# Handing out the attention's score steps in turn with the transposes and value products of other blocks

## The chip, the cores and the metric

The kernel runs on one core of one Trainium2 chip. A time is the device time of one execution in microseconds (us). The kernel before was timed three times: the median is 1233.09 us, the runs reach from 1231.47 to 1233.61. Engines are named as the profile names them: PE (matrix products), PEld (its weight loads), DVE (vector), ACT (scalar, activation functions), POOL (GpSimd) and SP (issues the DMAs).

## The reference

Two layers of a transformer trunk over a sequence of 512 tokens of width 1024, in float32. Each layer has two kinds of attention heads side by side, which share one input projection and one output projection, and then a dense MLP:

```python
proj = einsum('bsd,de->bse', rmsnorm(x, attn_norm[l]), w_in[l])
sb_q, sb_k, sb_v, df_q, df_k, df_v = split(proj, ...)      # 512 columns each
# stick-breaking: 8 heads of 64
z = q @ k.T * d**-0.5
log_keep = where(kpos < qpos, log_sigmoid(-z), 0.0)
between = cumsum(log_keep, reverse=True) - log_keep
w = where(kpos < qpos, exp(log_sigmoid(z) + between), 0.0)
sb_out = w @ v
# differential: 4 heads, two maps each of 64, values of 128, rotary positions on q and k
p = softmax(where(kpos // 64 <= qpos // 64, q @ k.T * d**-0.5, -inf))   # for both maps
df_out = rmsnorm((p[0] - lam * p[1]) @ v, subln_norm[l]) * (1 - lambda_init)
x = x + concat([sb_out, df_out]) @ w_o[l]
x = x + square(relu(rmsnorm(x, mlp_norm[l]) @ w_ff1[l])) @ w_ff2[l]
```

After both layers there is one final norm.

## The kernel before

Everything is held transposed, with features on the 128 partitions and the 512 tokens along the free axis. Each float32 operand of a product is split into a high part (rounded by ACT, `whi`, `h_hi`) and the remainder (by DVE, `wlo`, `h_lo`), and a product is three matmuls (function `three`, L255 to L260): high by high, and the two mixed ones. Weights come in units of 128 by 1024 numbers, loaded by SP (L106) and split one or two units ahead of use (L118 on ACT, L119 on DVE).

In each layer the attention is worked at the same time as the input projection. Two Python generators hand out work in steps. `dense()` (L693) goes through the projection's column blocks in the order d0, w0, d1, w1, ..., s0, u0, ...: d are queries and keys of a differential head, w its values, s and u the same of a pair of stick-breaking heads. One step of it is three matmuls of 512 columns (0.648 of the planner's units of cost). `attn()` (L652) yields attention steps with costs of 0.2 to 0.65. After each dense step the loop at L727 adds to a credit that is capped at 0.1, and while it is positive it takes the next attention step and subtracts its cost. A step that yields 0 is not ready: its queries and keys, or its values, are not due yet by the planner's clock, and the credit is dropped. Instructions recorded in this order are then ordered on each engine by the framework's scheduler, which follows this order by priority and its own notion of what is ready. On the chip each engine works through its own list in that order; waits are semaphores.

The attention of a layer is cut into 24 units: eight of the differential heads (4 heads times 2 halves of the queries) and sixteen of the stick-breaking heads (8 heads times 2 halves). A half has two query blocks of 128 tokens; block i sees 128(i + 1) keys. Work of a unit has three stages:

- `s1_df` or `s1_sb`, the scores: two matmuls into a PSUM bank of tag "s" (L487, L488), of which there are two. For a differential unit DVE then masks (L527, L531), takes the negated row maximum (L528, L532), ACT takes the exponential with its sum (L540), and DVE and POOL combine the two maps (L546 to L549). In the second half of a head (blocks 2 and 3) each map needs a bank of its own, so the unit has four score steps; in the first half two maps share one bank and there are two steps. For a stick-breaking unit ACT takes two sigmoids (L502, L503), DVE a product scan (L505) and POOL a product (L508); there are two steps.
- `s2`, the transposes of the weights: PE transposes (L568) into a bank of tag "t" (two banks, shared with the values' transposes vT, L393, and with the norm's rs and rb), then ACT and DVE split them (L205, L206: `zh`, `zl`, `fh`, `fl`). One step in the first half, two in the second.
- `s3`, the products with the values (L596 to L600) into the one bank of tag "o". One or two steps.

For unit i, `attn()` runs all score steps of unit i, then s2 of unit i - 2, then s3 of unit i - 3. When a differential head is complete its norm is put in between: `start_norm` (L639: transposes rs of L229, sums on DVE, a power on POOL at L236, a cast `chi` on DVE at L237, two diagonal products on POOL) and, one unit later, `finish` (L644: the broadcast matmuls rb of L251 and L252, then a split).

Projections are evicted by DVE; for queries and keys of a differential head POOL applies the rotation (L459, L460), ACT and DVE split the result (`h0d2k`, `l0d2k`), SP moves the pieces into stacked tiles (L425) and ACT copies others (L446, `copy_k`).

A tile's name has its layer and block: S0d230 is the score tile of layer 0, differential head 2, query block 3, map 0. The profile leaves out the number at the end.

Of the kernel before, what the change touches and what calls it, by code (L numbers as in the profile page):

```python
# [31 lines left out]
LAG2, LAG3, KSB = 2, 3, 7  # L32
# [54 lines left out]
class _Weights:  # L87
# [42 lines left out]
    def next(self, kind):  # L130
        i = self.used
        assert _UNITS[i][0] in kind
        self.used += 1
        if i > 0:
            self.do_split(i + 2)
        return self.tiles.pop(i)
# [3 lines left out]
def trunk(ctx, tc, xT, w, gains, lamv, cos, sin, out):  # L140
# [6 lines left out]
    def bank(tag, name, bufs=2):  # L147
        return ps.tile([P, 512], F32, tag=tag, name=name, bufs=bufs)
# [55 lines left out]
    def split(hi, lo, src):  # L204
        nc.scalar.activation(hi, src, AF.Copy)  # L205
        nc.vector.tensor_tensor(out=lo, in0=src, in1=hi.bitcast(F32), op=ALU.subtract)  # L206
# [41 lines left out]
    def rms_b(bc, name, dg):  # L248
        dg_hi, dg_lo = dg
        pb = bank("t", "rb_" + name)  # L250
        nc.tensor.matmul(pb, ones_r.to_broadcast([P, P]), dg_hi, start=True, stop=False)  # L251
        nc.tensor.matmul(pb, ones_r.to_broadcast([P, P]), dg_lo, start=False, stop=True)  # L252
        nc.scalar.copy(bc, pb)

    def three(pt, a, b, first, last):  # L255
        ah, al = a
        bh, bl = b
        nc.tensor.matmul(pt, ah, bh, start=first, stop=False)  # L258
        nc.tensor.matmul(pt, ah, bl, start=False, stop=False)  # L259
        nc.tensor.matmul(pt, al, bh, start=False, stop=last)  # L260
# [88 lines left out]
    for l in range(L):  # L349
        with ExitStack() as actx:  # L350
# [18 lines left out]
            def tt(name):  # L369
                return a2.tile([P, S], F32, tag="t", name=name, bufs=4)  # L370
# [184 lines left out]
            def s2(u):  # L555
                half = u["half"]
                nm = f"{l}{u['kind']}{u['b']}{u['m']}{half}"
                u["wT"] = {}
                for bk in range(half + 1):
                    zed = bk == half  # L560
                    pt = bank("t", f"T{nm}{bk}")
                    for kk in (1, 0):
                        kb = 2 * bk + kk
                        for qi in range(2):
                            if kb > 2 * half + qi:
                                continue
                            off = (1 - kk) * 256 + qi * P
                            nc.tensor.transpose(pt[:, off : off + P], u["w"][qi][:, kb * P : (kb + 1) * P], ident)  # L568
                    if zed:
                        zh, zl = zt[zn[0] % 2]  # L570
                        zn[0] += 1
                        a = 128
                    else:
                        zh = a2.tile([P, 512], F32R, tag="fh", name="fh" + nm, bufs=1)
                        zl = a2.tile([P, 512], F32R, tag="fl", name="fl" + nm, bufs=1)
                        a = 0
                    split(zh[:, a:512], zl[:, a:512], pt[:, a:512])
                    if not zed:
                        yield 0.44
                    for kk in range(2):  # L580
                        u["wT"][2 * bk + kk] = (
                            zh[:, (1 - kk) * 256 : (2 - kk) * 256], zl[:, (1 - kk) * 256 : (2 - kk) * 256])
                yield 0.33

            def s3(u):
                half, b, m, kind = u["half"], u["b"], u["m"], u["kind"]
                key = (kind, b, m)
                if half == 0:
                    heads[key] = bank("o", f"O{l}{kind}{b}{m}", 1)
                o = heads[key][:, half * 256 : half * 256 + 256]  # L590
                n = 2 * half + 2
                for kb in range(n):
                    wh, wl = u["wT"][kb]
                    if kind == "s":
                        v = vs[:, kb, 2 * b + m, :]
                        nc.tensor.matmul(o, v, wh, start=(kb == 0), stop=False)  # L596
                        nc.tensor.matmul(o, v, wl, start=False, stop=(kb == n - 1))  # L597
                    else:
                        three(o, (vd_hi[:, kb, b * P : (b + 1) * P], vd_lo[:, kb, b * P : (b + 1) * P]), (wh, wl),
                              kb == 0, kb == n - 1)  # L600
                    if kb % 2 and kb < n - 1:
                        yield 2 * 256 * (2 if kind == "s" else 3) * MMC
                if half == 1:
                    o = heads.pop(key)
                    if kind == "s":
                        if m == 0:
                            heads[("mt", b)] = a2.tile([P, S], F32, tag="mt", name=f"mt{l}{b}", bufs=MTB)
                        mt = heads[("mt", b)]
                        oc = tt(f"oc{l}{b}{m}")[0:64, :]
                        nc.scalar.copy(oc, o[64:128, :])  # L610
                        nc.vector.tensor_add(mt[64 * m : 64 * m + 64, :], o[0:64, :], oc)
                        if m == 1:
                            split(ms_hi[:, b, :], ms_lo[:, b, :], mt)
                    else:
                        os_ = a2.tile([P, S], F32, tag="mt", name=f"os{l}{b}", bufs=MTB)
                        sqo = tt(f"sqo{l}{b}")
                        nc.scalar.activation(sqo, o, AF.Square)
                        nc.scalar.activation(os_, o, AF.Copy, scale=gsub[:, l : l + 1])
                        rc = a3.tile([P, 4], F32, tag="rc", name=f"rc{l}{b}")
                        late.append((b, os_, sqo, rc))  # L620
                yield 2 * 256 * (2 if kind == "s" else 3) * MMC

            units = []
# [10 lines left out]
            def ok(key):  # L634
                return ready.get(key, 1e9) <= clock[0]
# [3 lines left out]
            def start_norm():  # L639
                b, os_, sqo, rc = late[0]  # L640
                dgs[b] = rms_a(sqo, 1.0 / P, rc, f"d{l}{b}", nc.gpsimd, tr)
                return 0.43

            def finish():  # L644
                b, os_, _, _ = late.pop(0)
                rb = tt(f"rb{l}{b}")
                rms_b(rb, f"d{l}{b}", dgs[b])
                nc.gpsimd.tensor_mul(os_, os_, rb)
                split(md_hi[:, b, :], md_lo[:, b, :], os_)
                return 0.43  # L650

            def attn():  # L652
                n = len(units)
                stage = 0
                for i in range(n + LAG3):
                    stage = stage + 1 if late else 0
                    if i < n:
                        u = units[i]
                        while not ok((u["kind"], u["b"])):
                            yield 0  # L660
                        yield from (s1_sb if u["kind"] == "s" else s1_df)(u)
                    if stage == 1:
                        yield start_norm()
                    if 0 <= i - LAG2 < n:
                        yield from s2(units[i - LAG2])
                    if stage == 2:
                        yield finish()
                        stage = 0
                    if 0 <= i - LAG3 < n:
                        while not ok(("v" + units[i - LAG3]["kind"], units[i - LAG3]["b"])):  # L670
                            yield 0
                        yield from s3(units[i - LAG3])

            def wo(half):
                for j in range(4):
# [17 lines left out]
            def dense():  # L693
# [28 lines left out]
                yield from wo(1)  # L722

            at = attn()
            done = spent = credit = 0.0
            live = True
# [23 lines left out]
        with ExitStack() as fctx:  # L750
# [25 lines left out]
            for half in range(2):  # L776
# [15 lines left out]
                n = HC - END if fin else HC  # L792
                for db in range(KC):
                    pt = bank("mm", f"f2_{l}{half}{db}", 3)
                    for s in range(2):
                        u = W.next("2")
# [72 lines left out]
```

## Time and profile before

| what | value |
|---|---|
| median of three runs | 1233.09 us |
| the profiled execution | 1232.63 us |
| its span, first to last instruction | 1230.8 us |
| PE busy in the span | 1196.4 us (97%) |
| DVE, ACT, POOL busy | 683.6, 550.6, 210.9 us |
| granted PE clock, mean | 0.993 |
| attention of layer 0 | about 55 to 210 us |
| attention of layer 1 | about 650 to 810 us |

A row of a timeline gives the start and the duration in us, the engine, the line of the kernel, the operation, the output and inputs by name, and in brackets how long the engine sat idle before it and what released it. A row of the waits gives who waited for whom, the total in us, the number of times and the longest. Ends of matmuls are modelled: consecutive rows of PE overlap, so their starts say more than their durations.

In the stretch from 55 to 105 us PE is busy for 43.65 of 50 us, from 160 to 200 us for 37.41 of 40. From 800 to 1200 us, in the MLP, it is busy throughout.

### The profile page before, as it was taken

The page shows a single profiled execution, that of the slowest core. Times are in us where ns is not written, and L with a number is a line of the kernel's source. Part 1 is how long each engine was busy: PE and PEld are TensorE (multiplying, and loading weights), DVE is VectorE, ACT ScalarE, POOL GpSimd, SP SyncE. Part 2 cuts the span into 40 slices and gives each one's busy share as a digit, 9 for nine tenths or more (in the row PEclk, how much of TensorE's full clock was granted, in tenths as well). Part 3 has the DMA queues.
Part 4 walks back from the last instruction along what each step waited for, and adds up shares of the span by engine and source line. Part 5 has one row for each costly group of instructions (what it writes and reads, how often), then busy time and mean ns, then how long its engine had stood idle before and what let it go on. Part 6 is the DMA issues. An engine that isn't in the chain of part 4 may idle for free.

```text
span 1230.8 us, 15320 instructions
## 1 busy us (share of the span) xinstructions
PE 1196.4 (97%) x5658; PEld 989.4 (80%) x5658; DVE 683.6 (56%) x1009; ACT 550.6 (45%) x932; POOL 210.9 (17%) x267
## 2 busy tenths in 40 slices
PE   8999999999999999999998999999999999999996
PEld 4777888888888888888887788788888888888886
DVE  6687878765442244443367787887644323444325
ACT  5666566544332134333246765665443221433214
POOL 4223453230000000001123244432200000000002
PEclk9999999999999999999999999999999999999998
DMA  6444444123322323323324343432232233233221
GB/s 198 114 142 121 115 134 122 59 86 103 103 88 101 103 88 101 103 87 102 103 84 141 105 134 107 129 92 84 86 103 99 90 103 95 93 103 91 90 94 69
DMA packets 46890, 128.16 MB, mean 104 GB/s; under 512 B 7264, under 2 KB 10336, under 8 KB 46816
## 3 DMA queue, kind: packets, MB, share of 16 engines
q1 hardware_dynamic: 46672, 127.17, 33.8%
q8 instruction: 45, 0.74, 0.2%
q14 instruction: 29, 0.24, 0.1%
q10 hardware_dynamic: 144, 0.02, 0.0%
HBM read 104.09 MB, written 2.10 MB: 86 GB/s over the span
## 4 chain that ended last, share of the span: by engine, by line
PE 87%; DVE 4%; ACT 3%; POOL 2%; issue 1%; DMA 1%; SPq 0%; DVEq 0%; POOLq 0%; ACTq 0%
PE f L258 19%; PE f L259 19%; PE f L260 19%; PE wo L259 2%; PE wo L258 2%; PE wo L260 2%; DVE wlo L119 1%; PE T1s L568 1%; PE T0s L568 1%; ACT p0d L540 1%; PE O1s L597 0%; PE O0s L597 0%; PE O0s L596 0%; PE O1s L596 0%; PE S1d L487 0%
## 5 line engine op out<-in xcount | busy, mean ns | idle before, releaser
L118 ACT ACTIVATE whi<-raw 128x1024 fp32r<-128x1024 f32 (+2 forms) x200 | 205.1, 1027 | 493.3 <-PE f L259 427.6
L119 DVE TENSOR_TENSOR wlo<-raw,whi 128x1024 fp32r<-128x1024 f32 (+2 forms) x200 | 247.7, 1239 | 151.6 <-ACT whi L118 150.5
L258 PE MATMUL f<-h_hi,whi 128*128 128x512 f32 x512 | 199.4, 389 | 0.0
L260 PE MATMUL f<-h_hi,wlo 128*128 128x512 f32 x512 | 199.2, 389 | 0.0
L259 PE MATMUL f<-h_lo,whi 128*128 128x512 f32 x512 | 199.2, 389 | 0.0
L258 PE MATMUL f<-uh,whi 128*128 128x512 f32 x496 | 192.9, 389 | 0.0
L259 PE MATMUL f<-ul,whi 128*128 128x512 f32 x496 | 192.9, 389 | 0.0
L260 PE MATMUL f<-uh,wlo 128*128 128x512 f32 x496 | 192.9, 389 | 0.0
L771 DVE SCALAR_TENSOR_TENSOR ft<-f,rbc 128x512 f32<-128x512 f32 x64 | 44.3, 692 | 163.9 <-PE f L260 163.0
L258 PEld LDWEIGHTS f<-h_hi,whi 128*128 128x128 f32 x512 | 96.1, 188 | 20.0
L260 PEld LDWEIGHTS f<-h_hi,wlo 128*128 128x128 f32 x512 | 96.1, 188 | 20.0
L259 PEld LDWEIGHTS f<-h_lo,whi 128*128 128x128 f32 x512 | 96.1, 188 | 19.8
L223 POOL TENSOR_TENSOR ssq<-ssq,sq 128x512 f32<-128x512 f32 x28 | 44.5, 1591 | 382.1 <-ACT sq L222 372.7
L260 PEld LDWEIGHTS f<-uh,wlo 128*128 128x128 f32 x496 | 93.1, 188 | 19.5
L258 PEld LDWEIGHTS f<-uh,whi 128*128 128x128 f32 x496 | 93.1, 188 | 19.3
L259 PEld LDWEIGHTS f<-ul,whi 128*128 128x128 f32 x496 | 93.1, 188 | 19.2
L800 DVE TENSOR_TENSOR x<-x,f 128x512 f32<-128x512 f32 x32 | 22.0, 688 | 103.0 <-PE f L260 103.0
L340 POOL TENSOR_TENSOR ssq<-ssq,sqf 128x256 f32<-128x256 f32 x6 | 4.4, 738 | 338.4 <-ACT sqf L338 335.0
L206 DVE TENSOR_TENSOR ul<-fu,uh 128x512 fp32r<-128x512 f32 x64 | 44.1, 692 | 0.4 <-ACT uh L205 0.4
L205 ACT ACTIVATE uh<-fu 128x512 fp32r<-128x512 f32 x64 | 40.6, 634 | 2.0
L772 ACT ACTIVATE fu<-ft 128x512 f32<-128x512 f32 x64 | 39.6, 618 | 1.6 <-DVE ft L771 1.6
L508 POOL TENSOR_TENSOR sig0s<-sig0s,C0s 128x128 f32<-128x128 f32 (+3 forms) x32 | 30.1, 939 | 55.0 <-DVE C0s L505 39.0
(722 smaller groups left out, 2164.9 us busy)
## 6 DMA issues: line engine op xcount, KB each, us to landing
raw<-in_w SPq DMA_DIRECT2D x176, 512.0 KB, 3.4
raw<-in_w SPq DMA_DIRECT2D x16, 448.0 KB, 3.2
x<-in_xT SPq DMA_DIRECT2D x8, 256.0 KB, 4.5
out_xT<-y SPq DMA_DIRECT2D x8, 256.0 KB, 2.4
raw<-in_w SPq DMA_DIRECT2D x8, 128.0 KB, 4.5
cos_t<-in_cos SPq DMA_DIRECT2D x2, 256.0 KB, 4.2
sin_t<-in_sin SPq DMA_DIRECT2D x2, 256.0 KB, 4.3
kl0d0k<-l0d0k SPq DMA_DIRECT2D x8, 64.0 KB, 2.2
```

Of the source, the lines that this page charges most:

```text
L118: nc.scalar.activation(hi[:, a:b], raw[:, a:b], AF.Copy)
L119: nc.vector.tensor_tensor(out=lo[:, a:b], in0=raw[:, a:b], in1=hi[:, a:b].bitcast(F32), op=ALU.subtract)
L205: nc.scalar.activation(hi, src, AF.Copy)
L206: nc.vector.tensor_tensor(out=lo, in0=src, in1=hi.bitcast(F32), op=ALU.subtract)
L223: eng.tensor_tensor(out=ssq, in0=ssq, in1=sq, op=ALU.add)
L258: nc.tensor.matmul(pt, ah, bh, start=first, stop=False)
L259: nc.tensor.matmul(pt, ah, bl, start=False, stop=False)
L260: nc.tensor.matmul(pt, al, bh, start=False, stop=last)
L508: nc.gpsimd.tensor_mul(sig[:, 0:wd], sig[:, 0:wd], C[:, 1 : wd + 1])
L568: nc.tensor.transpose(pt[:, off : off + P], u["w"][qi][:, kb * P : (kb + 1) * P], ident)
L771: nc.vector.scalar_tensor_tensor(out=t, in0=pt, scalar=0.0, in1=rbc, op0=ALU.max, op1=ALU.mult)
L772: nc.scalar.activation(uu, t, AF.Square)
```

## The change

The body of `attn()` is rearranged. What follows a unit's scores (the norm's start, s2 of unit i - 2, the norm's finish, s3 of unit i - 3) becomes a generator of its own, `behind_scores`. After each score step of unit i one step of that generator is handed out; what is left of it follows after the last score step. A step of it that is not ready yet (0) is asked again until it is. Which steps there are, their costs and what each computes stay as they are.

```diff
+            def behind_scores(i, stage):
+                n = len(units)
+                if stage == 1:
+                    yield start_norm()
+                if 0 <= i - LAG2 < n:
+                    yield from s2(units[i - LAG2])
+                if stage == 2:
+                    yield finish()
+                if 0 <= i - LAG3 < n:
+                    while not ok(("v" + units[i - LAG3]["kind"], units[i - LAG3]["b"])):
+                        yield 0
+                    yield from s3(units[i - LAG3])
+
             def attn():
...
                     stage = stage + 1 if late else 0
+                    rest = behind_scores(i, stage)
                     if i < n:
                         u = units[i]
                         while not ok((u["kind"], u["b"])):
                             yield 0
-                        yield from (s1_sb if u["kind"] == "s" else s1_df)(u)
-                    if stage == 1:
-                        yield start_norm()
-                    if 0 <= i - LAG2 < n:
-                        yield from s2(units[i - LAG2])
+                        front = (s1_sb if u["kind"] == "s" else s1_df)(u)
+                        for cost in front:
+                            yield cost
+                            nxt = 0
+                            while nxt == 0:
+                                nxt = next(rest, None)
+                                if nxt is not None:
+                                    yield nxt
+                    yield from rest
                     if stage == 2:
-                        yield finish()
                         stage = 0
-                    if 0 <= i - LAG3 < n:
-                        while not ok(("v" + units[i - LAG3]["kind"], units[i - LAG3]["b"])):
-                            yield 0
-                        yield from s3(units[i - LAG3])
```

A unit's steps are therefore handed out as score, transposes, score, transposes or values, ..., where they were score, score, transposes, ..., values.

## The prediction

> **What bounds the kernel now.** The page's busy shares come first: PE is busy 97% of 1230.8 us, so only PE's idle time can be won. I then asked for what PE waited for, over the span:
>
> ```profile
> PE S0d L487 <- ACT p0d L540: 6.7, 5, 2.2
> PE S1d L487 <- ACT p1d L540: 6.4, 4, 3.0
> ...
> PE rb_d L251 <- DVE zl L206: 2.0, 2, 1.0
> ...
> PE T0s L568 <- DVE vs L401: 1.6, 1, 1.6
> PE T1s L568 <- DVE vs L401: 1.6, 1, 1.6
> ...
> PE T0d L568 <- DVE p0d L549: 0.4, 1, 0.4
> ```
>
> Score matmuls of the differential blocks ("d") wait for a score bank that an exponential has not read out (13.1 us). A broadcast matmul rb and a transpose T of the stick-breaking blocks ("s") wait for a "t" bank (5.2 us). All are in the attention stretches. Third, the timelines around the largest waits say why:
>
> ```profile
> 99.38 0.48 PE L258 MATMUL p0w3v<-h_hi,whi 128*128 128x512 f32 x1
> 102.10 0.50 PE L487 MATMUL S0d<-st0d2k,st0d2q 128*128 128x512 f32 x1 [2.23 <-ACT p0d L540]
> 98.78 0.63 ACT L205 ACTIVATE h0d3k<-u0d3q 128x512 fp32r<-128x512 f32 x1 [2.67 <-POOL u0d3q L459]
> 99.45 1.90 ACT L446 ACTIVATE st0d3k<-h0d3k 32x512 fp32r<-32x512 f32 x3
> 101.38 0.58 ACT L540 ACTIVATE p0d<-S0d,sm0d 128x384 f32<-128x384 f32 x1
> 96.43 2.32 POOL L459 TENSOR_TENSOR u0d3q<-u0d3q,v0d3k 128x512 f32<-128x512 f32 x1
> ```
>
> The exponential itself takes 0.58, but ACT works in order: it sat 2.67 us for POOL's rotation, then made three copies, and PE waited.
>
> ```profile
> 186.66 0.48 PE L258 MATMUL p0s3q<-h_hi,whi 128*128 128x512 f32 x1
> 186.98 0.39 PE L259 MATMUL p0s3q<-h_lo,whi 128*128 128x512 f32 x1
> 189.69 0.55 PE L568 MATMUL T0s<-edge,sig0s 128*128 128x128 f32 x3 [1.62 <-DVE vs L401]
> 187.31 1.75 DVE L505 TENSOR_TENSOR_SCAN C0s<-keep0s,edge 128x512 f32<-128x512 f32 x1
> 188.97 0.66 DVE L401 TENSOR_TENSOR vs<-vT0u,vs 128x512 fp32r<-128x512 f32 x1
> 166.69 1.95 DVE L119 TENSOR_TENSOR wlo<-raw,whi 128x1024 fp32r<-128x1024 f32 x1
> 168.57 0.54 DVE L206 TENSOR_TENSOR zl<-T0s,zh 128x384 fp32r<-128x384 f32 x1
> ```
>
> In the s blocks it is DVE's order: the small splits that free a bank stand behind a scan (1.75) or a weight split (1.95).
>
> The idle column understates a wait, since the end of the matmul before it is modelled. I count start to start: 512-column matmuls follow each other every 0.23 us, so 99.38 to 102.10 loses 2.72 - 0.23 = 2.49.
>
> **What is lost now where the change reaches.** Layer 0, block d1 (68 to 81 us): 1.49 at 69.98, 0.23 at 72.08, 0.56 at 74.61, 0.26 at 80.97, sum 2.54. d2: 0.49 at 96.17 and 2.49, 2.98. d3: 1.09 at 125.68. Layer 1: d1 0.98 (676.49), d2 2.25 (702.06), d3 0.69 (723.60). s blocks: 1.15 at 169.26 and 1.79 at 189.69, and the same at 769.36 and 789.79, 5.88. Together **16.4 us**. The first pair of wide scores of block d0 (1.90 idle at 59.89, 3.00 at 656.14) is issued before any transposes are due; its surroundings keep their order, so both waits stay.
>
> **The change, part by part.** Nothing is added or removed: each engine has as many instructions (PE 5658 matmuls), and SP issues as many DMAs; only order moves. Direct costs are therefore zero, with the matmul stream itself as cover, and everything is in the waits. SP still issues the 16 stack moves of a block in one group (0.59 each), past at most one weight load more or less; no PE wait names these moves now, and scores follow them by several us: nothing. Walking the built program's new order with the durations above gives:
>
> *s blocks (16 units a layer).* The first transposes of a unit now come before its second score. At 169.26 the split zl now stands ahead of the eviction t0s2q (0.68) and the weight split (1.95) on DVE, and the norm's transposes are 1.8 us of PE work earlier, so POOL's power (1.0) no longer holds the cast behind it back: wait 0 instead of 1.15. At 189.69 T now takes a bank freed by a split that stands before the 1.75 scan: the copy, the weight split and a 384-wide scan still precede it, leaving 0.6 instead of 1.79. Two layers: 1.2 instead of 5.88. The closest new spacing of two score tiles on one bank is 4.5 us (4.9 before) against a sigmoid pair of 0.6 + 0.6, so these add nothing; if ACT were held up, the cover is 3 us.
>
> *d2.* Scores of a pair now stand 2.2 us apart on PE instead of 0.6 to 1.0, with transposes and the norm between. Layer 0: the second score's maximum now waits on DVE behind the cast chi, which waits for POOL's power (1.0) behind the rotation (2.32 beside DVE work); its exponential then ends 0.85 after PE arrives. Further on, weight split 13 falls behind that block's last combination (0.74) and PE's s0k projection waits 0.9. Sum 1.75, against 2.98. Layer 1's order has the maximum before chi and the weight split before the exponential: 0.3, against 2.25.
>
> *d3.* The second exponential goes behind a transposes' split zh on ACT, and rb behind the sigmoid table load (1.28): 0.3 + 0.35 in each layer, 1.3 against 1.78.
>
> *d1.* Here the change speaks against itself. Layer 0: the 1.49 goes, because the rotation's copies move behind the exponentials. But v0d2k is formed later, so POOL's rotation (1.3) runs ahead of the last map's scaling (1.04) and DVE's combination (0.74): the next transposes wait 1.55, where they waited 0.56. Then the block's third wide score comes only 1.6 us of PE work after the first (2.7 before), which is what memset, maximum and exponential take (0.11 + 0.55 + 0.58 + 0.19) without any queue. On ACT a weight split (1.09) and two 0.6 splits are ahead: 1.15. Its partner follows 4.1 us later and still finds 4 copies and a weight split ahead: 0.65. Small ones (whi 0.4, others 0.45) make 4.2 against 2.54. Layer 1: ACT waits for the rotation u1d2q (2.3 beside a weight split) ahead of the exponential: 1.35 + 0.4 = 1.75 against 0.98.
>
> Sum after: 1.2 + 1.75 + 0.3 + 1.3 + 4.2 + 1.75 = **10.5**. Gain 16.4 - 10.5 = **5.9 us**. The profiled execution took 1232.63 (span 1230.8 + 1.8 around it), the median shown is 1233.09, 0.46 above. So 1232.6 - 5.9 = 1226.7 by the profile and **1227 us** as median.
>
> Each remaining wait could be 0 (bank already free) or twice its size (two queues late together): after between 0 and 21, time between 1216.7 and 1237.7. I take the walked values, since their rows are neighbours of the ones moved.
>
> [...] The granted clock was 0.50 from 657.0 to 660.4, right after the 3.00 us idle; matmuls came every 0.43 there, which cost 1.5 us. No wait walked above reaches 3 us, so the sum has no such stretch besides this one. [...]
>
> POOL's L459 took 1.30 at 67.30, and DVE's combination that began 0.08 later took 1.63 (0.60 at 82.56, with POOL idle); at 96.43, begun 0.04 after a weight split on DVE, L459 took 2.32. I used 2.3 in layer 0's d2. [...]
>
> **Rivals.**
> - *The waits only change place* (1230.5 to 1235.5): the s gain of 4.7 holds, but d1 to d3 lose 4.7 more than their 10.5 of now. For: d1 already loses more by my walk. Against: d2's large waits have a named cause that moves away.
> - *Slower, about 1236.* ACT and DVE are in order, and transposes' splits and the norm's cast now stand between the two exponentials of a pair. If this holds PE at every d1 to d3 as long as the longest wait of this kind seen (3.00 idle, 3.16 start to start), the six lose 19.0, plus 1.2 in s: 20.2 - 16.4 = +3.8, hence 1236.9; with a single 3 us wait that halves the clock, +1.5 more. It decides from a mean of (16.4 - 1.2) / 6 = 2.5 us a block. For: d1 of layer 0 is above that by my walk. Against: elsewhere the pair's spacing doubles.
> - *Everything opens up*: no d wait is left, 1.2 in s: 1233.1 - 15.2 = 1218. Against it speaks the 1.6 us spacing in d1.
> - *The words do nothing*: the instruction scheduler reorders by its own readiness and PE's order stays. Excluded from d1 on: PE's order differs through both attention stretches.
>
> **How the numbers follow.** Under 0.2% (2.5 us) a measurement of this kernel hardly tells from no change; the three runs span 2.1. Forecast (2.5 to 10 us faster) 0.55, everything opens up 0.08, waits only change place 0.15, slower 0.22. Faster 0.63, same 0.15, slower 0.22. The forecast alone: 1223 to 1230.5. Range for 8 in 10: 1221 to 1235.5, leaving out half of the best case and the worst third of the slower one.
>
> **What would show it.** In the new profile: no PE wait of rb_d for zl in either layer; T0s for a split under 1 us; d2's wait under 1 us in layer 1; a transposes' wait T0d for p0d of about 1.5 and score waits at d1; the 1.9 and 3.0 of d0 as before. Wrong would be: a 2 us score wait left in d2 or d3, a second stretch at clock 0.5, or weight splits ("wlo") as new releasers of projections over 1 us.

## The result, and the profile after

The changed kernel takes 1230.83 us (median of ten executions, 1228.94 to 1233.19), the kernel before in the same sitting 1234.14. The ratio is 0.9974, with a 95% interval from 0.9965 to 0.9983: 3.2 us faster, between 2.1 and 4.3. The forecast was 5.9 us and a time of 1227.

The profiled execution of the changed kernel is its slowest, 1233.19 us with a span of 1231.4. The waits of PE in it, by the view that the prediction began with (who waited for whom: us, times, longest):

```profile
PE S1d L487 <- ACT p1d L540: 4.2, 2, 3.0
PE S0d L487 <- ACT p0d L540: 3.6, 3, 2.0
...
PE rb_d L251 <- DVE vs L401: 1.6, 2, 0.8
...
PE T0d L568 <- DVE p0d L549: 1.3, 2, 1.1
...
PE rb_d L251 <- DVE vdl L401: 1.0, 1, 1.0
PE p0s0k L260 <- DVE wlo L119: 0.8, 1, 0.8
PE T0s L568 <- DVE fl0s L206: 0.7, 1, 0.7
...
PE T1s L568 <- DVE fl1s L206: 0.4, 1, 0.4
```

Waits of scores for exponentials fell from 13.1 to 7.8 us, and those for `zl` and for `vs` at T0s and T1s (5.2) are gone. New are rb behind the values' splits `vs` and `vdl` (2.6), transposes behind the combination (1.3, was 0.4), a weight split (0.8) and T behind `fl` (1.1). Start to start, in the prediction's blocks (every place is counted at which PE starts 0.13 us or more late):

| block | before | forecast | after |
|---|---|---|---|
| layer 0, d1 | 2.54 | 4.2 | 3.16 |
| layer 0, d2 | 2.98 | 1.75 | 2.12 (1.14 score, 0.98 weight split) |
| layer 0, d3 | 1.09 | 0.65 | 1.81 (0.98 of it rb) |
| layer 1, d1 | 0.98 | 1.75 | 1.61 |
| layer 1, d2 | 2.25 | 0.3 | 1.53 (1.16 of it rb) |
| layer 1, d3 | 0.69 | 0.65 | 1.82 (0.98 of it rb) |
| s blocks, both layers | 5.88 | 1.2 | 2.06 |
| sum | 16.4 | 10.5 | 14.1 |

So the s blocks gave 3.8 us and the differential blocks took 1.5 back: 2.3 by waits (2.0 with those of head 0), at the lower end of the measured interval. Head 0's first wide scores wait as before (2.13 and 3.17 start to start; 2.06 and 3.16).

The clock differs too. In the windows table of the changed kernel (stretch, its length, busy time and instructions of PE, PEld, DVE, ACT and POOL, granted clock, DMA share and GB/s):

```profile
58.44:61.85 3.41, 1.44 (x7) 1.01 (x7) 2.72 (x9) 2.97 (x10) 0.54 (x2) 1.00 0.38 96
61.85:65.27 3.42, 3.42 (x10) 2.75 (x9) 3.31 (x8) 0.67 (x2) 1.38 (x1) 0.50 0.44 102
652.36:655.77 3.41, 1.25 (x6) 0.71 (x4) 1.44 (x3) 3.36 (x6) 0.00 (x0) 1.00 0.41 104
655.77:659.18 3.41, 2.56 (x7) 2.37 (x8) 1.55 (x7) 3.36 (x12) 1.02 (x2) 0.50 0.43 108
659.18:662.60 3.42, 3.42 (x10) 2.57 (x10) 2.19 (x5) 1.90 (x4) 0.83 (x1) 0.50 0.33 76
```

There are three half-clock stretches in the attention where before had one, and two where it had one at the start (17.48 to 24.31); each costs 1.5 to 1.8 us in the attention. This execution therefore took longer than the profiled one of before (1232.63) although it waited less. The clock varies from one execution to the next: the ten have mean clocks from 0.989 (1233.19 us) to 0.995 (three of them, 1228.94 to 1229.08); those of the kernel before in the later sittings have 0.990 to 0.995.

### The profile page after: what moved, and what is told of

It reads as the page before. It is cut to its first block, busy times and chain, and to the rows that moved or that the text cites. A ratio compares the mean times of both kernels' runs of the same rounds, so it can differ in the third digit from the quotient of the medians.

```text
span 1231.4 us, 15317 instructions
## 1 busy us (share of the span) xinstructions
PE 1201.3 (98%) x5658; PEld 992.8 (81%) x5658; DVE 679.6 (55%) x1009; ACT 551.2 (45%) x932; POOL 208.7 (17%) x267
## 4 chain that ended last, share of the span: by engine, by line
PE 80%; DVE 6%; ACT 5%; POOL 3%; issue 2%; DMA 1%; SPq 0%; DVEq 0%; POOLq 0%; ACTq 0%
PE f L260 19%; PE f L258 19%; PE f L259 19%; PE wo L258 2%; PE wo L260 2%; PE wo L259 2%; DVE wlo L119 1%; ACT whi L118 1%; PE T1s L568 1%; DVE C0s L505 0%; SPq L425 0%; PE T0s L568 0%; ACT p0d L540 0%; PE O1s L597 0%; PE O1s L596 0%
## 5 line engine op out<-in xcount | busy, mean ns | idle before, releaser
L508 POOL TENSOR_TENSOR sig1s<-sig1s,C1s 128x128 f32<-128x128 f32 (+3 forms) x32 | 26.8, 837 | 55.2 <-DVE C1s L505 36.8
```

What stands on the lines that cost most here:

```text
L508: nc.gpsimd.tensor_mul(sig[:, 0:wd], sig[:, 0:wd], C[:, 1 : wd + 1])
```

## Experiments

Ratios are to the kernel before, measured in the same sitting, with the 95% interval (its medians there were 1232.36 to 1234.14, so medians of different sittings are not compared). Traces are compared by their waits, which depend less than the time on where a half-clock stretch falls; they are summed start to start as above, over the attention of both layers, half-clock slowness listed apart:

| kernel | median, us | ratio (interval) | waits in the attention | half-clock there |
|---|---|---|---|---|
| before | 1234.14 | 1 | 21.6 | 1.8 |
| changed | 1230.83 | 0.9974 (0.9965 to 0.9983) | 19.6 | 4.9 |
| s units alone | 1229.36 | 0.9973 (0.9962 to 0.9984) | 18.5 | 3.0 |
| d units alone | 1235.08 | 1.0010 (1.0000 to 1.0020) | 20.8 | 1.5 |
| end of the norm last | 1232.46 | 0.9989 (0.9980 to 0.9998) | 20.3 | 1.7 |
| head 0 later | 1232.11 | 0.9988 (0.9979 to 0.9997) | 20.4 | 1.8 |
| s units and head 2 | 1232.90 | 0.9989 (0.9979 to 0.9999) | 19.0 | 4.9 |
| key copies on POOL | 1233.26 | 0.9998 (0.9988 to 1.0009) | 22.9 | 1.8 |
| key copies on DVE | 1237.25 | 1.0032 (1.0020 to 1.0044) | 26.1 | 0 |
| key copies as transfers | 1235.72 | 1.0019 (1.0010 to 1.0028) | 25.0 | 1.8 |
| norm's start after products | 1245.23 | 1.0096 (1.0081 to 1.0111) | 27.9 | 10.7 |
| norm's start after transposes | 1234.81 | 1.0016 (1.0006 to 1.0025) | 22.9 | 5.2 |
| norm with other tiles | 1230.47 | 0.9978 (0.9966 to 0.9991) | 19.9 | 1.8 |
| s units, head 1's copies on POOL | 1225.18 | 0.9939 (0.9925 to 0.9952) | 15.8 | 0 |
| both, head 1's copies on POOL | 1227.26 | 0.9951 (0.9938 to 0.9963) | 17.1 | 0 |

The waits and the half-clock loss are of the one profiled execution of each, which need not be a typical one.

**One kind of unit alone.** The first theory, A, was that the missing gain sits in the new waits for a t bank; its rival, B, that it sits in half-clock stretches.

```diff
-                            nxt = 0
+                            nxt = 0 if u["kind"] == "s" else None
```

> Only the sixteen stick-breaking units are handed out in turn; the eight differential units go score, score, transposes as before. Theory A (the gain that is missing sits in new waits for a t bank: in the changed kernel's trace rb waits 0.98 in each layer in the first stick-breaking unit, T 0.95 and 0.64 later, about 0.7 of small ones; before, these places lose 5.88): the s blocks are worth 5.9 - 4.3 = 1.6 us, so about 1232.5 against 1234.1 before (ratio 0.9987). By the walk of the prediction they are worth 4.7: 1229.4 (0.9962). Theory B (the changed order as such brings more half-clock stretches): the stretch at 61.9 to 65.3 lies ahead of these units, so B says 4.7 as well.

Measured 0.9973, a gain of 3.3 us (2.0 to 4.7): the stick-breaking units alone have all that the whole change has. A, which gave them 1.6 us, is contradicted; their trace has 2.4 us of waits in these units and no rb among them.

```diff
-                            nxt = 0
+                            nxt = 0 if u["kind"] == "d" else None
```

> Only the eight differential units are handed out in turn; the stick-breaking units as before. Theory A: waits of d1 to d3 after, from the changed kernel's trace, are 9.6 to 10.8 where they were 10.5 (the rb of the first norm in layer 1 at 715 us, 1.16, is new): between 0.9 faster and 0.3 slower, about 1233.8 (ratio 0.9997). By the prediction's walk 1.2 faster: 1232.9. Theory B (more half-clock stretches from the changed order of the d units): 1.5 to 3 slower, 1235.6 to 1237.

Measured 1.0010 (1.0000 to 1.0020): the differential units in turn gain nothing, and cost some 1.2 us if anything. Their waits are 11.9 in the trace (10.5 before). The interval (0 to 2.5 us slower) leaves room for A's upper end (0.3) and for the lower end of B (1.5). The trace does not decide it: it is of the fastest of the twelve executions (1231.15), with one half-clock stretch in the attention, as before, and over the whole attention it waits less than before (20.8, was 21.6), since the stick-breaking units, handed out as before, lose 3.6 instead of 5.9. Whether waits or clock make the median slower stays open.

**The rb waits.** The end of the norm was moved behind the value products.

```diff
-                if stage == 2:
-                    yield finish()
                 if 0 <= i - LAG3 < n:
...
                     yield from s3(units[i - LAG3])
+                if stage == 2:
+                    yield finish()
```

> The changed kernel, but the end of a differential head's norm (the broadcast rb and what follows) is handed out after the value products of that unit instead of ahead of them. Theory A: the three rb waits of the changed kernel (0.98 at 138 us, 1.16 at 715 us, 0.98 at 739 us) are gone, since by then the splits of the values have freed the t bank: 3.1 us faster than the changed kernel, 1227.7 (ratio to before 0.9948). Theory B (the missing gain is in half-clock stretches): no change against the changed kernel, 1230.8 (0.9974). Third way: a transposes step meets the same bank instead, 1230 to 1231, and T takes rb's place in the list of waits.

Measured 0.9989: slower than the changed kernel (the two intervals just overlap), nearest to the third way, though above its range, and it is a score, not T, that takes rb's place. The timelines of the changed kernel and of this one at the place of the largest rb wait:

```profile
713.29 0.69 DVE L430 SCALAR_TENSOR_TENSOR t1s0q<-p1s0q,rbc 128x512 f32<-128x512 f32 x1
...
713.89 0.68 DVE L206 TENSOR_TENSOR l1d3k<-v1d3q,h1d3k 128x512 fp32r<-128x512 f32 x1
...
714.52 0.69 DVE L401 TENSOR_TENSOR vdl<-vT1w,vdh 128x512 fp32r<-128x512 f32 x1
...
715.36 0.47 PE L251 MATMUL rb_d<-dghd,ones_r 128*128 128x512 f32 x1 [0.99 <-DVE vdl L401]
```

```profile
715.71 0.47 PE L487 MATMUL S1d<-st1d3k,st1d3q 128*128 128x256 f32 x2 [0.99 <-DMA st1d3q<-l1d3k]
```

Without rb there, PE stops for the same 0.99 us at a score of head 3, whose stack is moved from `l1d3k`. Both waits have one source: `l1d3k` and `vdl` come late on DVE, one behind the other. The t bank is only where the lateness shows, and A is dropped.

**Head 0 handed out later.**

```diff
                         while not ok((u["kind"], u["b"])):
                             yield 0
+                        if i == 1:
+                            for _ in range(15 if l else 7):
+                                yield 0
```

> The changed kernel, but the second half of head 0 is handed out later: 7 more projection steps in layer 0 and 15 in layer 1 are asked for first, which puts 14 and 18 more projection matmuls (3.2 and 4.1 us) ahead of its first wide score in PE's order. Both theories: the waits of 2.0 and 3.0 us there are gone, 5.3 us, and with them the half-clock stretches behind them, of which the profiled execution had three of 3.4 us, each worth 1.4 to 1.5 us. Theory B: all of the spread between runs goes too and the time is about 1221.5 to 1223 (ratio 0.990). Theory A with the clock an accident of the runs: between 1222 and 1225.5. If PE only meets the same wait later or the attention ends later by what was put ahead: 1229 to 1231, no gain.

Measured 0.9988: no gain. PE reached the first wide score late enough, and met the same exponentials at the next ones, then projections that waited for weight splits, and transposes:

```profile
64.20 0.50 PE L487 MATMUL S0d<-st0d0k,st0d0q 128*128 128x512 f32 x1 [1.26 <-ACT p0d L540]
...
66.20 0.50 PE L487 MATMUL S0d<-st0d0k,st0d0q 128*128 128x512 f32 x1 [0.58 <-ACT p0d L540]
...
654.71 0.50 PE L258 MATMUL p1d2k<-h_hi,whi 128*128 128x512 f32 x1 [1.21 <-ACT whi L118]
...
656.34 0.50 PE L260 MATMUL p1d2k<-h_hi,wlo 128*128 128x512 f32 x1 [0.90 <-DVE wlo L119]
...
670.66 0.55 PE L568 MATMUL T1d<-edge,p1d 128*128 128x128 f32 x3 [1.73 <-DVE p1d L549]
```

**Block by block, or ACT's backlog (theory C).**

```diff
-                            nxt = 0 if u["kind"] == "s" else None
+                            nxt = 0 if u["kind"] == "s" or u["b"] == 2 else None
```

> The stick-breaking units and, of the differential ones, head 2 alone are handed out in turn; heads 0, 1 and 3 as before. Theory A (each wait belongs to the place where the order puts two instructions, and can be bought block by block): of the run with the stick-breaking units alone, the waits of 0.49 + 2.50 (layer 0) and 2.23 (layer 1) at head 2 become what the changed kernel has there, 1.14 + 0.98 and 0.37 + 1.16: 1.6 us less, about 1227.8 (ratio 0.9960). Theory C (in the d blocks ACT's and DVE's own backlog sets how long PE waits, and the order only decides at which instruction): the same total, 1229 to 1230 (0.997).

By time inconclusive (0.9989; the mean clock was 0.989 in seven of twelve executions). By the trace the waits of heads 1 to 3 are 11.2 where the s units alone have 10.7: nothing was bought in the sum. Head 2's own scores wait less (1.4 and 1.3 us in the two layers, 3.0 and 2.3 in the run with the s units alone), but transposes, rb and head 3's scores wait more.

Then ACT was relieved of the key copies, by POOL (`nc.gpsimd.tensor_copy`), by DVE (`nc.vector.tensor_copy`) and by transfers:

```diff
-                return lambda: nc.scalar.activation(dst, src.bitcast(F32), AF.Copy)
+                return lambda: nc.gpsimd.tensor_copy(dst, src.bitcast(F32))
```

> The changed kernel with the eight copies of rotated keys of each differential head (32 by 512, 0.63 each on ACT, 5 us a head) made by POOL. Theory C: with 40 us less on ACT in all, the waits at head 0 (2.1 and 3.3) shrink by the copies ahead of the exponentials (1.9 and 3.2) and those of heads 1 to 3 (12.1 in the trace) by a third or more: 6 to 8 us, 1223 to 1225 (0.992). Theory A (order of the banks): head 0 alone, 4 to 5 us and the half-clock stretch behind it. If POOL takes 1 us or more for a copy, the rotations (2.2) queue behind eight of them and scores come late: 1231 or more.

> The same with DVE making the copies. Theory C: ACT loses 40 us, DVE gets 0.3 to 0.6 each, 20 to 40 us; head 0's waits fall as with POOL, the others move from exponentials to DVE's maxima and splits: 3 to 6 us less than the changed kernel, 1225 to 1228. Theory A: 4 to 5 us.

```diff
-                                defer(KC_GAP * (4 * j + 2 * m + i + 1), copy_k(k[d_, m, :], hi[rk, :]))
+                                move(k[d_, m, :], hi[rk, :])
```

> The same with the copies as transfers, eight more a head on SP's queue (0.6 us each to issue there). Theory C: as with POOL, 6 to 8 us less than the changed kernel, 1223 to 1225, as ACT and POOL are both free. If 24 issues a head hold up the weight loads behind them on SP (14 us a head where it was 9.5, a weight unit every 5 to 6 us), projections wait for weights: 1235 or more.

All three are slower than the changed kernel (0.9998, 1.0032, 1.0019). ACT's busy time from 50 to 140 us fell from 60.4 us to 46.1, 42.7 and 42.9, and head 0's wait in layer 0 from 2.13 to 0.54 with POOL. But heads 1 to 3 lose 17.3 there (12.1 in the changed kernel), with new waits at head 3's scores (the waits of the run with POOL; "issue" means that the profile shows nothing that released it):

```profile
PE S0d L487 <- issue: 2.9, 1, 2.9
...
PE S1d L487 <- DMA st1d3q<-l1d3k: 2.4, 1, 2.4
```

With transfers the scores' waits for exponentials did fall, from 7.8 to 2.6 us, but transposes wait 4.1 for the combination, and projections wait for weight splits; ACT itself waits 4.2 us for a weight to arrive between 50 and 140 us, which it does not in the changed kernel. So for POOL and for the transfers the last case of the expectation is what came. The forecasts of C are contradicted: less load on ACT did not shorten the sum of the waits. Each of the three runs also loads another queue, so they do not show what ACT's load would do alone.

**The lists that the scheduler makes (theories E and F).** One engine at a time kept its list in the order in which the kernel records its instructions.

```diff
-MAN = ()
+MAN = ("DVE",)
```

The other runs have `"Activation"` or `"PE"` in its place.

> The changed kernel with DVE's list left in the order in which the kernel records its instructions; the framework's scheduler still orders the other engines. Theory E (the waits of the d blocks come from head-of-line blocking in lists that the scheduler makes by its own idea of what is ready: at 713.3 DVE evicts p1s0q, for which it had to sit idle, ahead of a split l1d3k that had been ready for 3 us): the waits of this kind go and the d blocks lose 6 to 9 instead of 12.1, 1225 to 1228 (ratio 0.994). Theory F (DVE, busy 69 of 90 us there, is loaded so far that any order leaves the same waits): 1230 to 1232. If the scheduler's order lets evictions overtake blocked instructions, the recorded one is worse: above 1236.

> The same with ACT's list in the recorded order. Theory E: the copies of keys and splits that stand ahead of exponentials go behind them where they are recorded later; the score waits (3.6 and 4.2 us in all, 5.4 of them at head 0) shrink by a third to a half: 1226 to 1229 (0.995). Theory F: no change, 1230 to 1232. Worse, above 1236, if the recorded order puts exponentials, which wait for DVE's maxima, ahead of weight splits that projections need.

> The same with PE's list in the recorded order, so that the steps stand exactly where the planner hands them out, one or two projection steps (0.7 us each) between two attention steps. Theory E: the scheduler had placed each score and transposes as soon as it took them for ready; in recorded order they come at even distances, and the d blocks lose less than 12.1: 1226 to 1229. Theory F: 1230 to 1232. If even distances are shorter than the chains of maximum, exponential, scaling and combination (3 us and more), PE waits at every step: 1240 or more.

> PE's list in the recorded order, with the stick-breaking units handed out in turn and the differential ones a unit at a time. Against the run with both in turn and PE in recorded order it shows what the change does to the differential blocks when nothing re-sorts PE. By the words of the change, in turn gives twice the distance between two scores of a bank, so this one is slower by 3 us or more; by theory E's scheduler alone there is no reason for a difference above 2 us.

Measured: DVE 1.0727 (1.0708 to 1.0747), ACT 1.0338 (1.0319 to 1.0356), PE 1.0242 (1.0221 to 1.0263), PE with only the s units in turn 1.0150 (1.0131 to 1.0169). The scheduler's sorting is worth 30 to 90 us here: the recorded order is no cure, so E in the form tested is contradicted, and so is F, for which any order would do. The surprise is the last pair: unsorted, the differential units in turn are 11 us slower than a unit at a time (1262.78 and 1251.72), in part by the clock (ten half-clock stretches in the attention against seven; mean clocks of the profiled executions 0.981 and 0.986). The waits with both kinds in turn, then with the s units alone:

```profile
PE S0d L487 <- DMA st0d3q<-l0d3k: 6.1, 1, 6.1
PE S0d L487 <- ACT p0d L540: 5.4, 4, 2.9
PE S1d L487 <- DMA st1d3q<-l1d3k: 5.0, 1, 5.0
PE S1d L487 <- ACT p1d L540: 3.0, 2, 1.7
```

```profile
PE S0d L487 <- ACT p0d L540: 10.3, 6, 4.3
PE S1d L487 <- ACT p1d L540: 5.4, 5, 2.3
```

Waits for exponentials are halved (15.7 to 8.4), and PE waits 11.1 us for the transfers of head 3's stacks. The trace of the scheduled kernels has the same lateness. Head 3's second split piece, the norm's first diagonal product (`dghd`) and head 3's first score, before and after:

```profile
102.61 0.63 ACT L205 ACTIVATE h0d3k<-v0d3q 128x512 fp32r<-128x512 f32 x1
...
104.41 0.68 DVE L206 TENSOR_TENSOR l0d3k<-v0d3q,h0d3k 128x512 fp32r<-128x512 f32 x1
...
106.62 1.04 POOL L241 TENSOR_TENSOR dghd<-edge,chi 128x512 fp32r<-128x512 f32 x1 [0.34 <-DVE sm0d L546]
...
111.74 0.28 PE L487 MATMUL S0d<-st0d3k,st0d3q 128*128 128x256 f32 x1
```

```profile
102.96 1.04 POOL L241 TENSOR_TENSOR dghd<-edge,chi 128x512 fp32r<-128x512 f32 x1 [0.28 <-DVE chi L237]
...
104.00 0.62 ACT L205 ACTIVATE h0d3k<-u0d3q 128x512 fp32r<-128x512 f32 x1
...
110.83 0.63 ACT L205 ACTIVATE h0d3k<-v0d3q 128x512 fp32r<-128x512 f32 x1
...
113.92 0.68 DVE L206 TENSOR_TENSOR l0d3k<-v0d3q,h0d3k 128x512 fp32r<-128x512 f32 x1
...
117.37 0.40 PE L487 MATMUL S0d<-st0d3k,st0d3q 128*128 128x256 f32 x2
```

The piece is 9.5 us later. The pieces `h` and `l` live in four tiles (`tr`, tag "hl"), and `start_norm` takes two of the same four for its diagonal products `dghd` and `dgld`. In the kernel before these are recorded behind head 3's pieces, in the changed one, where the norm's start follows the first score at once, ahead of them (`dghd` at 106.62 and at 102.96). With two tiles left, the second pieces would have to wait for the copies and transfers of the first. That is theory H; its rival I is that every order leaves the same sum of waits. By H the split `l1d3k` of 713.89, which theory E took for ready, was waiting for its tile.

**The norm's start and its tiles.**

```diff
-                if stage == 1:
-                    yield start_norm()
                 if 0 <= i - LAG2 < n:
                     yield from s2(units[i - LAG2])
+                if stage == 1:
+                    yield start_norm()
```

This is the run after the transposes; in the other the two lines follow `s3`.

> The changed kernel, but the start of a head's norm is handed out last in its unit, behind the value products, instead of right behind the first score. Theory H (the norm's two diagonal products take two of the four tiles that hold the split pieces; in the changed kernel they are recorded ahead of head 3's pieces, so the second half of these has to wait for the copies and transfers of the first: l0d3k at 113.9 us where it was 104.4, scores of head 3 at 117.4 instead of 111.7): the pieces are on time again, rb's 1.16 in layer 1 and the waits at head 3 shrink, d waits 10 instead of 12.1: 1228.5 to 1229.6 (ratio 0.9960). Theory I (any order of these steps leaves the same total of waits in the d blocks, only elsewhere): 1230.8 (0.9974).

> The same with the norm's start behind the transposes and ahead of the value products. Theory H: as the other place, 1228.5 to 1229.6. Theory I: 1230.8. The difference between the two places, if any, is that of the norm's rs and rb among the t banks, under 1 us.

```diff
+            def dg_tile(name):
+                return a2.tile([P, S], F32R, tag="ks", name=name, bufs=KSB)
...
-                dgs[b] = rms_a(sqo, 1.0 / P, rc, f"d{l}{b}", nc.gpsimd, tr)
+                dgs[b] = rms_a(sqo, 1.0 / P, rc, f"d{l}{b}", nc.gpsimd, dg_tile)
```

> The changed kernel with its order of steps, but the norm's two diagonal products are put among the seven tiles of the weights (p, keep, sig) instead of the four of the pieces. Theory H: the same gain without moving a step, 1228.5 to 1229.6, and h0d3k's second half within 5 us of the first. If the seven tiles are as tight: exponentials wait for a tile, 1232 or more. Theory I: 1230.8.

And the norm's start after the transposes with PE in recorded order:

> Both kinds of units in turn, the norm's start behind the transposes, PE's list in the recorded order. Theory H: of the run with PE in recorded order and both kinds in turn (1262.8), the waits of head 3's first scores for their stacks (9.1 and 8.0 us) go, 1244 to 1248, and so in turn beats a unit at a time (1251.7) in the differential blocks, whose score waits it halves (8.4 against 15.7). If head 3 is handed out too early for another reason: 1260 to 1263.

H's mechanism is there. With other tiles and no step moved, `h0d3k`'s second piece starts 1.8 us behind the first (98.40 and 100.20) where it was 6.8 (104.00 and 110.83), and in layer 1 heads 1 to 3 lose 3.55 instead of 4.96, with neither of the rb waits of 1.16 and 0.98. In layer 0 rb still waits 0.71 (0.98 in the changed kernel). With PE in recorded order the 6.1 and 5.0 are gone and 1262.78 becomes 1247.47, less than the 1251.72 of a unit at a time; the waits for exponentials, though, are 9.1 and 4.0 there, so that most of their halving had been the lateness of the stacks. And the gain that H promised is not there: with other tiles the ratio is 0.9978 and the waits are 19.9, as without them (0.9974, 19.6), which is what I says. What came instead, from the timelines of ACT and of PE in the kernel with other tiles:

```profile
98.40 0.63 ACT L205 ACTIVATE h0d3k<-u0d3q 128x512 fp32r<-128x512 f32 x1 [3.62 <-POOL u0d3q L462]
...
100.20 0.63 ACT L205 ACTIVATE h0d3k<-v0d3q 128x512 fp32r<-128x512 f32 x1
...
102.78 0.58 ACT L543 ACTIVATE p0d<-S0d,sm0d 128x384 f32<-128x384 f32 x1
```

```profile
103.50 0.50 PE L490 MATMUL S0d<-st0d2k,st0d2q 128*128 128x512 f32 x1 [3.26 <-ACT p0d L543]
```

With the pieces on time ACT sits 3.62 us for POOL's rotation ahead of an exponential, and PE waits 3.26 (3.42 start to start): the wait of 2.49 that the change had taken from block d2 is back, larger. With the tiles of the changed kernel the scheduler has head 3's pieces behind that exponential (104.00 after 103.43), with others ahead of it. In the s blocks the waits grew from 2.1 to 3.8. Moving the norm's start back is worse than either (1.0016, 1.0096): rb then waits for POOL (2.06 at 140 us in the one, 2.87 at 139 us in the other).

**One cause on one queue.** Head 0's waits, among the largest of both kernels, stand behind head 1's key copies on ACT (in layer 1 five of 0.63, then a table load of 1.28). These eight copies alone went to POOL.

```diff
-            def copy_k(dst, src):
+            def copy_k(dst, src, b):
+                if b == 1:
+                    return lambda: nc.gpsimd.tensor_copy(dst, src.bitcast(F32))
                 return lambda: nc.scalar.activation(dst, src.bitcast(F32), AF.Copy)
...
```

> The stick-breaking units alone in turn, and of the key copies only the eight of head 1 on POOL, which stand on ACT ahead of head 0's exponentials (five of 0.63 each in layer 1). If a wait can be bought where its cause is one queue: head 0's waits of 2.1 and 3.3 become 0.5 and 2.5 as with all copies on POOL, and half-clock stretches behind them get rarer, 2.5 to 4 us less than without it (1229.4): 1225 to 1227 (ratio 0.9935). Theory I (any order or relief leaves the same sum of waits in the d blocks): 1229 to 1231.

> The changed kernel with the same eight copies of head 1 on POOL: 1227 to 1228.5 (0.995) if the waits are bought, 1230.8 or more by theory I.

Measured 0.9939 (0.9925 to 0.9952) and 0.9951 (0.9938 to 0.9963): 7.5 and 6.0 us faster than before. Head 0's waits are 2.7 in all instead of 5.4, those of heads 1 to 3 stay (10.7 and 12.0), and no half-clock stretch is left in the attention. In layer 1, from the timelines of the first of the two:

```profile
645.92 6.08 POOL L447 CAST st1d1k<-h1d1k 32x512 fp32r<-32x512 f32 x8 [0.73 <-ACT h1d1k L205]
...
648.32 1.28 ACT L542 ACT_TABLE_LOAD   x1 [1.94 <-DVE sm1d L534]
```

POOL has nothing else to do in these 6 us (in the changed kernel it sits idle there for 7.60 us, up to 656.85), and ACT is free for the table load as soon as DVE has the maxima. So I does not hold where a wait has one cause on one queue with room beside it. The version with a unit at a time for the differential heads is the faster by its median and by its waits; the two intervals overlap.

## Why the prediction was right and wrong

**Right.** The direction. PE is the bound and all is in its waits: as many matmuls, direct costs nil. *s blocks*: rb's wait for `zl` is gone in both layers, and T waits 0.95 and 0.64 for `fl` (0.6 was said for each layer); the walk's 4.7 us came out at 3.8 in the trace, and the run of these units alone gains 3.3 (2.0 to 4.7). *d1*: in layer 0 the waits for the combination (1.25, 1.55 was said) and for the third wide score (0.88, 1.15 was said) are where they were expected, and in layer 1 the wait behind the rotation (1.32, 1.35 was said). *Layer 0, d2*: the maximum behind `chi` (1.14, 0.85 was said; POOL's rotation ahead of it began 0.17 behind a weight split on DVE and took 2.20, 2.3 was used) and the split of weight 13 (0.98, 0.9 was said). Head 0's waits are unchanged.

**Wrong in its size.** The failing steps are the terms "d3" (0.65 in each layer) and "d2, layer 1" (0.3), which measured 1.81, 1.82 and 1.53: 5.2 us instead of 1.6. With 0.9 more in the s blocks, 0.4 more in d2 of layer 0 and 1.2 less in d1 that is the 3.6 us by which the sum was off; that d1 was put too high hides a part of the miss, and that is luck. Most of the three terms is rb: it waits 0.98, 0.98 and 1.16, 3.1 us in all, where the prediction had 0.35 in each d3, put down to the sigmoid table load, and nothing in d2 of layer 1. The rows name the splits of the values on DVE instead (`vs` twice, `vdl`).

Why these splits come late is shown for layer 1. The step that failed there is the sentence on the moved steps, "no PE wait names these moves now, and scores follow them by several us: nothing". It looked at transfers and queues and not at the tiles. The norm's start, moved to the first score, takes two of four tiles ahead of head 3's pieces, the second of which then comes some 9.5 us later; in layer 1 it stands on DVE just ahead of `vdl`, and rb waits. In the run with other tiles the pieces are on time and both of layer 1's rb waits are gone. In layer 0 rb still waits 0.71 of its 0.98 there, so the tiles are not its main cause, and why `vs` is late stays open. The tiles alone do not give the time back either: in the same run head 2's scores wait 3.42 and 1.95 us, where they waited 1.14 in layer 0 and not at all in layer 1. The change's gain in d2 and its loss behind it are two sides of one placement on ACT, as far as these rows show.

**The rivals.** What happened is nearest to "the waits only change place" (1230.5 to 1235.5), at its edge: the greater part of the s gain holds, and the differential blocks lose more than before, though by 1.5 us and not the 4.7 named. "Slower" would have needed 2.5 us a block; the mean is 2.0. Against the 1233.09 from which the prediction started, 1230.83 is 2.3 us less.

**The clock.** "No wait walked above reaches 3 us, so the sum has no such stretch besides this one" is wrong as a rule. A wait of 2.13 us at 60.58 was followed by such a stretch; the wait of 2.06 at the same place before was not. The prediction had named a second stretch at clock 0.5 as a sign of being wrong, and it came; d2's wait under 1 us in layer 1, a sign of being right, did not (1.16, at rb). Which stretches an execution has is known only for the profiled ones: the old one at 657 us doubled in the changed kernel and is absent in the run with the norm's end last. The executions of the changed kernel differ by 4 us, more than the change gains, and the slower ones have the lower mean clock.

## What to carry to other kernels

When a step is moved earlier, look at every ring of tiles from which it allocates, not only at the queues: with two tiles taken ahead of another user, that user came 9.5 us later, with no new wait at the moved step itself. When a wait goes, ask which delay removed it; here the gain in one block went with the lateness of the next. Relieve one queue of the one thing that a named wait stands behind, where another engine is idle, rather than relieve an engine altogether: eight copies a layer gave 4 us with the s units alone (0.9973 to 0.9939) and 3 with the whole change (0.9974 to 0.9951); all thirty-two cost 3 (0.9974 to 0.9998).

## What was not expected of the hardware

In both traces the half-clock stretches lie on a grid of their own. In the changed kernel's they last 3.41 us, or 6.83 where two follow each other, and 61.85 and 655.77 lie 44.37 and 638.29 us (13 and 187 times 3.413) behind 17.48, where the first of them began. In before's the second (656.99) lies 638.29 us behind the first (18.70). Counted from the first instruction, the two grids are 1.2 us apart. PE was not idle all through the stretch ahead of a half-clock one: the changed kernel's rows above were followed by half clock with PE busy 1.44 and 1.25 us of 3.41. In the run with the norm's end last the longest wait for an exponential (3.0 us of idle time) falls into two stretches of 3.41, with PE idle 1.69 and 1.30 us in them, and the clock stays whole:

```profile
652.27:655.68 3.41, 1.72 (x8) 1.10 (x6) 1.88 (x6) 3.37 (x5) 0.00 (x0) 1.00 0.44 110
655.68:659.09 3.41, 2.11 (x10) 1.74 (x11) 1.77 (x9) 3.40 (x11) 1.01 (x2) 1.00 0.39 97
```

With head 0 later, a stretch with two waits of 1.37 and 1.07 us was followed by half clock:

```profile
653.88:657.29 3.41, 1.68 (x7) 1.16 (x8) 2.52 (x6) 3.33 (x5) 0.61 (x1) 1.00 0.39 97
657.29:660.70 3.41, 3.41 (x10) 2.84 (x9) 3.41 (x8) 0.71 (x2) 0.00 (x0) 0.50 0.75 225
```

With the attentions of before and of the changed kernel (50 to 830 us) cut at each one's own grid, the full-clock stretches followed by half clock are those with PE busy 0.85 us (before), 1.25 and 1.44 (changed); all others have 1.75 or more. Ahead of the attention 1.70 (before) and 1.81 (changed) were followed by half clock. In other runs 0.81 (d units alone), 1.40 (s units alone), 1.51 (key copies on POOL) and the 1.68 above were; 1.57 (key copies on DVE), 1.68 (d units alone), 1.72 (norm's end last) and 1.74 (key copies on POOL) were not. So in these numbers, in which the ends of matmuls are modelled, PE's busy time alone does not part the two. Half-clock stretches that are themselves not full were followed by another at 2.56 (655.77 to 659.18) and 2.67 (17.48 to 20.89) in the changed kernel and at 2.43 with the s units alone, but not at 3.02 with the d units alone or at 3.27 in before (18.70 to 22.11).

The key copy of 32 by 512 took 0.63 us on ACT each time (before and changed kernel), 0.42 mostly and up to 1.40 on DVE, and 0.60 to 1.70 on POOL (the runs with all key copies there).
